# Branch A's values: split fp32r products of one head against unsplit fp32 products of two heads on the two column halves of the array

## The chip, the cores and the metric

The kernel runs on one core of one Trainium2 chip. The metric is the device time of the whole program in microseconds (us), the median of several runs. Shorter is better. The engines are TensorE (PE in the profile, its weight loads PEld), VectorE (DVE), ScalarE (ACT), GpSimd (POOL) and SyncE (SP), which here issues all transfers.

## The reference

One layer of an encoder with two token-mixing branches is applied to two groups (prompt and sample) of 1024 tokens and 1024 channels, with the same weights. Cut to what matters here:

```python
h = rms_norm(x, norm_g) * (1 + scale) + shift
qa, ka, va, za, qb, kb, vb, zb, ga, gb = split(h @ w_in)
# branch A: 8 query heads, 2 key/value heads, 64 dims each
qa, ka = rope(rms_norm(qa)), rope(rms_norm(ka))
p  = softmax(qa @ ka.T / 8)            # for each of 8 heads, 1024 x 1024
oa = (p @ va) * silu(za)               # four query heads share one va
# branch B: 4 heads, two 64-dim softmax maps each, 128-dim values
pd = softmax(q0 @ k0.T / 8) - lam * softmax(q1 @ k1.T / 8)
ob = rms_norm(pd @ vb) * (1 - lam_init) * silu(zb)
merged = sigmoid(ga) * (oa @ w_proj_a) + sigmoid(gb) * (ob @ w_proj_b)
y = x + gate * (merged @ w_out)
```

## The kernel before

Everything is fp32 in and out. Most matrix products are made of fp32r operands that were split in two: a rounded part (an ACT copy to fp32r) and the remainder (a DVE or POOL subtraction), with two or three matmuls for one product. Branch B's values (line 810) are an exception: `WHOLE` is true for both of its pairs of heads, and they use plain fp32 operands in one matmul each.

The two groups run one after the other. Each has a head (keys, values and the first queries of branch A), then six phases of attention, then gates, projections and the output. Phases 0 and 1 are branch A's heads 0 to 3 and 4 to 7, which share key/value head 0 and 1; phases 2 to 5 are branch B's heads. During a phase the attention's steps are woven with projections: `qa_gen`, `qkb_gen` and `vb_gen` (line 497) and `z_gen` (line 679), which store the gate paths. `weave` takes steps in proportion to tables of weights; a scheduler then orders each engine's instructions by simulated time and priority, and attention steps are given a raised priority.

Branch A's attention before works in **units**: one head and 256 queries, 32 units a group. A unit has two score tiles of 128 queries by 1024 keys. For each, four matmuls (lines 709 and 710) fill a double bank of PSUM, DVE takes the maximum (711), ACT the exponential into a tile p (712), of which there are four; DVE transposes p in 32 x 32 blocks (745); and four transfers (750) bring it as pieces into a tile q. So q holds the 256 queries' weights with keys on partitions; it is `pair()`, with two buffers.

The values follow `BEHIND` 1.4 units later, in `a_values`. `pT_pieces` goes over q in four pieces: ACT copies a piece to fp32r into a tile hi (758), DVE subtracts in place (759). For each of eight chunks of 128 keys there are then two matmuls of 128 x 256: va's rounded part (columns 0 to 63) and its remainder (64 to 127) are the stationary operand, hi (770) and the rest in q (771) the moving one. Rows 0 to 63 of the result a and rows 64 to 127 are summed at the end by an ACT copy of one half (786) and a DVE addition (787), and a transfer stores 64 rows (791). There is one buffer for a.

A score tile of the unit after next needs a free p, p is free when its transfers into q are done, and those wait until q is no longer read by line 771. All transfers are issued in order by SP.

Of the kernel before, what the change touches and what calls it, by code (L numbers as in the profile page):

```python
# [20 lines left out]
P = 128  # L21
T = 1024
D = 1024
NCH = D // P
# [40 lines left out]
BEHIND = 1.4  # L65
AHEAD = 100
PV_LAG = 2

WHOLE = (True, True)
# [21 lines left out]
def kernel(ctx: ExitStack, tc: tile.TileContext, t: dict):  # L91
# [8 lines left out]
    qpool = ent(tc.tile_pool(name="qpool", bufs=2))  # L100
    tpool = ent(tc.tile_pool(name="tpool", bufs=2))
# [450 lines left out]

    def pipelined(ht, w, front, back):
        pend = []
        for tt in range(NTT):
            ps = yield from proj_tt(ht, w, tt)
            pend.append((tt, front(tt, ps)))
            if len(pend) > LAG:
                back(*pend.pop(0))
            yield 1  # L560
        while pend:
            for _ in range(1 if alone[0] else 3):
                yield 1
            back(*pend.pop(0))
        yield 1
# [79 lines left out]
    def vb_gen(ht, out, pr):  # L645
        w = load_w(w_cols(w_in, (C_VB + pr * 256, 256)))
        if WHOLE[pr]:
            v = utile().bitcast(F32).rearrange("p (n h e) -> p n h e", n=NTT, h=2)
            out[2 * pr], out[2 * pr + 1] = v[:, :, 0], v[:, :, 1]
        else:  # L650
            vs = [utile().rearrange("p (n s e) -> p n s e", n=NTT, s=2) for _ in range(2)]
            out[2 * pr], out[2 * pr + 1] = vs
        for tt in range(NTT):
            ps = yield from proj_tt(ht, w, tt)
            if WHOLE[pr]:
                nc.scalar.activation(v[:, tt].rearrange("p h e -> p (h e)"), ps, AF.Copy)
                yield 1
                continue
            for i in range(2):
                vp = ps[:, i * P : (i + 1) * P]  # L660
                nc.scalar.activation(vs[i][:, tt, 0, :], vp, AF.Copy)
                nc.vector.tensor_tensor(
                    out=vs[i][:, tt, 1, :], in0=vp, in1=vs[i][:, tt, 0, :].bitcast(F32), op=ALU.subtract
                )
            yield 1
# [51 lines left out]
    def scores(u, i):  # L717

        nm_ = len(u["q"])
# [5 lines left out]
        su = u["su"][:, qt : qt + 1] if m == 0 else tiny.tile([P, 1], F32, tag="su", name=nm("su"))  # L725
        softmax_unit(u["q"][m][:, qt * P : (qt + 1) * P], u["sw"][:, m, t * P : (t + 1) * P], u["k"][m], pt, su)
        if m == 0:
# [8 lines left out]
        return t if m == nm_ - 1 else None  # L736

    def flip(u, t):


        pt = u[t][0]
        if len(u[t]) > 1:
            _, p1, f = u[t]
            nc.vector.scalar_tensor_tensor(out=pt, in0=p1, scalar=f, in1=pt, op0=ALU.mult, op1=ALU.add)
        nc.vector.transpose(pt, pt)  # L745
# [6 lines left out]
    def pT_pieces(u):  # L752

        pT = u["pT"].rearrange("p (q c b) -> p c q b", q=8, c=8)
        for cc in range(4):
            tl = pT[:, cc * 2 : cc * 2 + 2]
            th = tpool.tile([P, 2, 8, 32], F32R, tag="hi", name=nm("hi"), bufs=3)
            nc.scalar.activation(th, tl.bitcast(F32), AF.Copy)  # L758
            nc.vector.tensor_tensor(out=tl, in0=tl.bitcast(F32), in1=th.bitcast(F32), op=ALU.subtract)  # L759
            yield cc, th, tl  # L760

    def a_values(u):
        acc = ps_a.tile([P, 512], F32, tag="a", name=nm("a"))[:, :256]
        ready = []

        def pv(cc, th, tl):
            for c in range(2):
                k = cc * 2 + c
                lt = u["v"](k)
                nc.tensor.matmul(acc, lt, th[:, c, :], start=(k == 0), stop=False)  # L770
                nc.tensor.matmul(acc, lt, tl[:, c, :], start=False, stop=(k == 7))  # L771

        for piece in pT_pieces(u):
            ready.append(piece)
            if len(ready) > PV_LAG:
                pv(*ready.pop(0))
            yield 1
        while len(ready) > 1:
            pv(*ready.pop(0))
            yield 1  # L780
        pv(*ready.pop())
        tmp = mtile("at", [P, 256], bufs=1)
        o = mtile("oo", [P, 256])
        j = u["j"]
        a, b = (slice(0, 64), slice(64, 128)) if j % 2 == 0 else (slice(64, 128), slice(0, 64))
        nc.scalar.activation(tmp[a], acc[b], AF.Copy)
        nc.vector.tensor_tensor(  # L787
            out=query_order(o[a]), in0=piece_order(acc[a]), in1=piece_order(tmp[a]), op=ALU.add
        )
        pr = u["pr"]  # L790
        dma(u["od"][pr // 2][a, (pr % 2) * 256 : (pr % 2 + 1) * 256], o[a])
        yield 1

    def b_values(u):
        acc = ps_a.tile([P, 512], F32, tag="a", name=nm("a"))[:, :256]
        ready = []
        def pv(cc, th, tl):
            for c in range(2):
                k = cc * 2 + c
                for s, rt in ((0, th), (0, tl), (1, th)):  # L800
                    nc.tensor.matmul(
                        acc, u["v"][:, k, s, :], rt[:, c, :],
                        start=(k == 0 and s == 0 and rt is th), stop=(k == 7 and s == 1),
                    )

        if WHOLE[u["h"] // 2]:
            pT = u["pT"].bitcast(F32).rearrange("p (q c b) -> p c q b", q=8, c=8)
            yield 1
            for k in range(NCH):
                nc.tensor.matmul(acc, u["v"][:, k], pT[:, k], start=(k == 0), stop=(k == 7))  # L810
                if k % 2:
                    yield 1
        else:
            for piece in pT_pieces(u):
                ready.append(piece)
                if len(ready) > PV_LAG:
                    pv(*ready.pop(0))
                yield 1
            while len(ready) > 1:
                pv(*ready.pop(0))  # L820
                yield 1
            pv(*ready.pop())
# [20 lines left out]
    def attention(units):  # L843
# [11 lines left out]
        for at, ph, n, i, qk in steps:  # L855
# [4 lines left out]
            with tc.high_priority(offset=AHEAD):  # L860
# [12 lines left out]
                if t is not None:  # L873
                    late.append(lambda u=live[n], t=t: flip(u, t))
                    if t == (0 if ph < 2 else 0) and n + 1 < len(units) and units[n + 1][2]():
# [140 lines left out]
    def units_of(st):  # L1016

        def a_unit(half, i, pr):
            j = half * 4 + i
            kv = j // 4  # L1020
            return {
                "q": [st["qa"][half][i % 2][:, i // 2]], "k": [st["ka"][:, kv]],
                "v": (lambda k: st["va"][:, k, kv, :]),
                "pr": pr, "j": j, "od": st["od"][j // 2], "su": st["suA"][:, j],
# [14 lines left out]
        for half in range(2):  # L1039
            units += [  # L1040
                (half, lambda a=(half, i, pr): a_unit(*a), lambda a=("qa", half, pr): there(*a))
                for i in (0, 2, 1, 3) for pr in range(4)
# [29 lines left out]
    for g in range(2):  # L1072
# [11 lines left out]
        def phase(k, *fs, more=()):  # L1084
            n_att = 16 * (6 + PV_LAG) if k < 2 else 4 * (9 + PV_LAG)
# [96 lines left out]
```

## Time and profile before

| | |
|---|---|
| median of 3 runs (lowest, highest) | 1984.54 us (1979.33, 1988.07) |
| span of the profiled execution | 1985.5 us, which is also the only time that the profile gives for it |
| mean granted TensorE clock | 0.982 |
| DMA | 295.11 MB, mean 149 GB/s |

A row of the profile's groups reads: line, engine, operation, output and inputs by the program's names, shapes and types, the count; then busy time in us and the mean of one in ns; then the time for which the engine was idle just before such instructions and what it waited for. Busy time counts overlapping instructions once. A matmul's duration contains its way through the array, so that two in a row overlap; how fast they follow one another is read from their starts or ends. In a row of the waits stand who waited for whom, the total in us, how often, and the longest.

Where PE's time goes, beside the lines shown with the prediction (busy us of the groups): line 679 582.3, line 497 487.0, lines 709 and 710 (scores) together 421.2, line 950 (projections after the gates) 187.2, line 979 (output) 178.6.

### The profile page before, as it was taken

How to read it: one execution, taken by the hardware profiler on the slowest of the kernel's cores; microseconds unless marked ns; L12 is line 12 of the kernel's file. 1: busy time of each engine (PE TensorE's matmuls, PEld its weight loads, DVE VectorE, ACT ScalarE, POOL GpSimd, SP SyncE). 2: the span in 40 equal slices, each digit the busy share in tenths (PEclk: the TensorE clock that was granted, in tenths of full speed). 3: DMA queues.
4: the chain of work that ended last, by engine and by line, in shares of the span. 5: the costliest groups of instructions: out<-in, count | busy, mean ns of one | idle time of the engine just before them, and what ended most of it. 6: DMA issues, size and time to landing. Idle time of an engine off the chain costs nothing.

```text
span 1985.5 us, 30670 instructions
## 1 busy us (share of the span) xinstructions
PE 1908.6 (96%) x10466; PEld 1627.8 (82%) x10466; DVE 1330.8 (67%) x1906; ACT 1009.9 (51%) x1939; POOL 758.1 (38%) x1008
## 2 busy tenths in 40 slices
PE   8889999999999998999999899999999999999999
PEld 3878888888878994778888787888887888877887
DVE  4558877777877577547465877677788845665641
ACT  4435655665654444754323565556655534566310
POOL 2374612453446252221235464134445626422110
PEclk9899999999999999999999999999999999999999
DMA  8124556555553345865641455565654333567532
GB/s 310 33 80 126 155 152 169 152 166 154 133 153 102 101 120 173 257 227 167 222 149 35 140 144 145 149 164 144 184 137 137 106 97 99 156 212 245 174 101 75
DMA packets 269531, 295.11 MB, mean 149 GB/s; under 512 B 35776, under 2 KB 218176, under 8 KB 269376
## 3 DMA queue, kind: packets, MB, share of 16 engines
q1 hardware_dynamic: 269376, 293.15, 49.7%
q8 instruction: 84, 1.38, 0.3%
q14 instruction: 71, 0.58, 0.1%
HBM read 133.59 MB, written 42.01 MB: 88 GB/s over the span
## 4 chain that ended last, share of the span: by engine, by line
PE 68%; DMA 8%; DVE 8%; ACT 5%; SPq 4%; issue 3%; POOL 3%; ACTq 0%; POOLq 0%; DVEq 0%
PE f L497 16%; PE f L679 16%; PE f L950 6%; PE f L979 5%; PE s L709 4%; PE a L810 4%; PE s L710 4%; PE s L979 4%; DMA q<-p 3%; SPq L750 3%; PE s L950 2%; DVE q L759 2%; PE a L771 2%; PE a L770 2%; DVE m L711 2%
## 5 line engine op out<-in xcount | busy, mean ns | idle before, releaser
L679 PE MATMUL f<-u,w 128*128 128x512 f32 x2232 | 582.3, 398 | 0.1
L497 PE MATMUL f<-w,u 128*128 128x256 f32 x3456 | 487.0, 286 | 2.2 <-ACT ev L685 1.4
L497 PEld LDWEIGHTS f<-w,u 128*128 128x128 f32 x3456 | 459.5, 192 | 22.4 <-ACT ev L685 1.8
L679 PEld LDWEIGHTS f<-u,w 128*128 128x128 f32 x2232 | 408.8, 190 | 77.3 <-POOL w L181 0.8
L181 POOL TENSOR_TENSOR w<-st,w 128x512 fp32r<-128x512 f32 x168 | 230.3, 1390 | 439.9 <-ACT w L179 375.1
L712 ACT ACTIVATE p<-s,m 128x1024 f32<-128x1024 f32 x256 | 284.4, 1111 | 206.3 <-DVE m L711 111.3
L711 DVE TENSOR_REDUCE m<-s 128x1 f32<-128x1024 f32 x256 | 310.0, 1216 | 51.3 <-PE s L710 48.7
L745 DVE STREAM_TRANSPOSE p<-p 128x1024 f32<-128x1024 f32 x192 | 238.2, 1241 | 99.2 <-ACT p L712 86.5
L759 DVE TENSOR_TENSOR q<-q,hi 128x512 fp32r<-128x512 f32 x256 | 198.3, 792 | 60.6 <-ACT hi L758 58.6
L515 POOL TENSOR_TENSOR rs<-ss,nhalf 128x4 f32<-128x4 f32 (+1 forms) x112 | 112.8, 1007 | 322.8 <-DVE ss L514 284.0
L758 ACT ACTIVATE hi<-q 128x512 fp32r<-128x512 f32 x256 | 153.8, 625 | 104.1 <-DMA q<-p 55.4
L710 PE MATMUL s<-u,sw 128*128 128x512 f32 x512 | 206.7, 404 | 0.0
L179 ACT ACTIVATE w<-st 128x512 fp32r<-128x512 f32 x196 | 113.9, 625 | 97.2 <-DMA st<-in_w_in_dram 46.0
L950 PE MATMUL f<-u,w 128*128 128x512 f32 x552 | 133.4, 395 | 5.1 <-ACT ev L685 4.4
L770 PE MATMUL a<-hi,u 128*128 128x256 f32 x512 | 132.5, 285 | 2.1 <-DVE oo L787 2.1
L771 PE MATMUL a<-q,u 128*128 128x256 f32 x512 | 129.8, 286 | 1.2 <-DVE q L759 1.2
L810 PE MATMUL a<-q,u 128*128 128x256 f32 x512 | 128.3, 390 | 1.9 <-DVE oo L826 1.5
L950 PEld LDWEIGHTS f<-u,w 128*128 128x128 f32 x552 | 103.9, 190 | 27.2 <-ACT ev L685 4.7
L709 PE MATMUL s<-u 128*128 128x512 f32 x256 | 110.9, 433 | 15.1 <-ACT p L712 15.1
L810 PEld LDWEIGHTS a<-q,u 128*128 128x128 f32 x512 | 97.8, 196 | 17.5 <-DVE oo L826 1.6
L709 PE MATMUL s<-u,u 128*128 128x512 f32 x256 | 103.6, 405 | 8.3 <-ACT p L712 7.7
L710 PEld LDWEIGHTS s<-u,sw 128*128 128x128 f32 x512 | 98.4, 192 | 15.5
(175 smaller groups left out, 2562.1 us busy)
## 6 DMA issues: line engine op xcount, KB each, us to landing
q<-p SPq DMA_DIRECT2D x768, 128.0 KB, 2.6
st<-in_w_in_dram SPq DMA_DIRECT2D x132, 256.0 KB, 3.0
zd<-ev SPq DMA_DIRECT2D x96, 256.0 KB, 2.2
sw<-u SPq DMA_DIRECT2D x256, 64.0 KB, 2.1
p<-zd SPq DMA_DIRECT2D x64, 256.0 KB, 3.2
u<-in_w_ada_dram SPq DMA_DIRECT2D x8, 1024.0 KB, 10.4
st<-in_w_in_dram SPq DMA_DIRECT2D x64, 128.0 KB, 2.7
st<-in_w_out_dram SPq DMA_DIRECT2D x32, 256.0 KB, 2.9
```

Source lines behind the costliest of these rows:

```text
L181: e.tensor_tensor(out=wl, in0=st, in1=wh.bitcast(F32), op=ALU.subtract)
L497: nc.tensor.matmul(ps, lt[c][:, sl], w[:, c, wi, :], start=(k == 0), stop=(k == 23))
L679: nc.tensor.matmul(ps, w[:, c, wi, e * P : (e + 1) * P], rt[c], start=(k == 0), stop=(k == 23),)
L709: nc.tensor.matmul(s[:, sl], q, k[:, sl], start=True, stop=False)
L710: nc.tensor.matmul(s[:, sl], sw, k[:, sl], start=False, stop=True)
L711: nc.vector.tensor_reduce(out=m, in_=s, axis=AX.X, op=ALU.max, negate=True)
L712: nc.scalar.activation(pt.rearrange("p (j c a) -> p j c a", j=4, c=8), s.rearrange("p (c a j) -> p j c a", c=8, j=4), AF.Exp, bias=m, accu ...
L745: nc.vector.transpose(pt, pt)
L759: nc.vector.tensor_tensor(out=tl, in0=tl.bitcast(F32), in1=th.bitcast(F32), op=ALU.subtract)
L810: nc.tensor.matmul(acc, u["v"][:, k], pT[:, k], start=(k == 0), stop=(k == 7))
L950: nc.tensor.matmul(ps, w[:, c, wi, d * P : (d + 1) * P], o[:, oi, :], start=(k == 0), stop=(k == 11))
L979: nc.tensor.matmul(ps, w[:, c, wi, e * P : (e + 1) * P], m[:, mi, :], start=(k == 0), stop=(k == 23))
```

## The change

Branch A's attention works in **couples** of units: two neighbouring query heads that share a key/value head, and 256 queries; 16 couples a group. A couple has four score tiles, two for each head, and a q tile for each head. There are three q buffers; the pool of hi is gone.

va is kept as plain fp32. A couple's result a has one head in rows 0 to 63 and the other in rows 64 to 127. For each of the eight chunks there are two matmuls with 64 columns of va as stationary operand and 256 columns of the one or the other head's q as moving operand, in fp32 without a split. The 16 are emitted in turn between the halves, and `together` binds them: each after the first gets a very high priority and a dependence, without a semaphore, on the one before it. The result is copied by one ACT instruction of 128 rows and stored by one transfer.

The path for split weights in branch B, which `WHOLE` had switched off, is deleted with its flag; branch B's instructions stay. Steps of the values in phases 0 and 1 become two for a couple (`PAIRS`: 1.05 couples behind, 0.3 apart over both), and the counts that `weave` divides by follow.

```diff
+PAIRS = (1.05, 0.3)
+TOP = 100000
-PV_LAG = 2
-WHOLE = (True, True)
...
-    qpool = ent(tc.tile_pool(name="qpool", bufs=2))
-    tpool = ent(tc.tile_pool(name="tpool", bufs=2))
+    qpool = ent(tc.tile_pool(name="qpool", bufs=3))
...
+    def behind(ins, other):
+        dep = mybir.DependencyInfo(mybir.DependencyClass.NoSync, mybir.DependencyReason.DATA)
+        tc.add_manual_dep(ins.ins, other.ins.name, dep)
+
+    def together(calls):
+
+        prev = None
+        for call in calls:
+            if prev is None:
+                ins = call()
+            else:
+                with tc.high_priority(offset=TOP):
+                    ins = call()
+                behind(ins, prev)
+            prev = ins
...
-        va = utile().rearrange("p (n k d) -> p n k d", n=NTT, k=2)
+        va = utile().bitcast(F32)[:, :1024].rearrange("p (n k d) -> p n k d", n=NTT, k=2)
...
-            vt = va[:, tt]
-            nc.scalar.activation(vt[:, :, 0:64], vp, AF.Copy)
-            nc.vector.tensor_tensor(out=vt[:, :, 64:128], in0=vp, in1=vt[:, :, 0:64].bitcast(F32), op=ALU.subtract)
+            nc.scalar.activation(va[:, tt], vp, AF.Copy)
...
-        t, m = i // nm_, i % nm_
+        pairs = "h" not in u
+        t, m = (i % 2, i // 2) if pairs else (i // 2, i % 2)
...
-            u["pT"] = pair(F32R)
-        dst = u["pT"].bitcast(F32).rearrange("p (i t f) -> p i t f", i=4, t=2)
+            pT = pair()
+            if "h" in u:
+                u["pT"] = pT
+            else:
+                u.setdefault("pT", []).append(pT)
+        dst = (u["pT"] if "h" in u else u["pT"][m]).rearrange("p (i t f) -> p i t f", i=4, t=2)
...
-    def pT_pieces(u):
-            nc.scalar.activation(th, tl.bitcast(F32), AF.Copy)
-            nc.vector.tensor_tensor(out=tl, in0=tl.bitcast(F32), in1=th.bitcast(F32), op=ALU.subtract)
...
     def a_values(u):
         acc = ps_a.tile([P, 512], F32, tag="a", name=nm("a"))[:, :256]
-                nc.tensor.matmul(acc, lt, th[:, c, :], start=(k == 0), stop=False)
-                nc.tensor.matmul(acc, lt, tl[:, c, :], start=False, stop=(k == 7))
...
-        nc.scalar.activation(tmp[a], acc[b], AF.Copy)
-        nc.vector.tensor_tensor(
-            out=query_order(o[a]), in0=piece_order(acc[a]), in1=piece_order(tmp[a]), op=ALU.add
-        )
+        pT = [x.rearrange("p (q c b) -> p c q b", q=8, c=8) for x in u["pT"]]
+        together([
+            lambda k=k, m=m: nc.tensor.matmul(
+                acc[(LO, HI)[m]], u["v"][:, k], pT[m][:, k], start=(k == 0), stop=(k == 7)
+            )
+            for k in range(NCH) for m in (1, 0)
+        ])
+        yield 1
         o = mtile("oo", [P, 256])
+        nc.scalar.activation(query_order(o), piece_order(acc), AF.Copy)
...
-            na, nv = (2, 4 + PV_LAG) if ph < 2 else (4, 5 + PV_LAG)
-            steps += [(n + i / na, ph, n, i, True) for i in range(na)]
-            steps += [(n + BEHIND + i / nv, ph, n, i, False) for i in range(nv)]
+            nv, after, pace = (2, *PAIRS) if ph < 2 else (7, BEHIND, 1.0)
+            steps += [(n + i / 4, ph, n, i, True) for i in range(4)]
+            steps += [(n + after + i * pace / nv, ph, n, i, False) for i in range(nv)]
...
-            n_att = 16 * (6 + PV_LAG) if k < 2 else 4 * (9 + PV_LAG)
+            n_att = 8 * 6 if k < 2 else 4 * 11
```

How PE's order changes at the first values of the first group. A row is line, operation, result and inputs with the numbers of their buffers (a is the values' result, f a projection's, u a kept tile, here va in u_397 and u_394, w a weight), output shape, and a count of equal rows in turn. Before, the middle of the first unit's 16 matmuls:

```order
L679 MATMUL f_1504<-u_553,w_1346 128x512
L771 MATMUL a_1568<-q_1546,u_397 128x256
L770 MATMUL a_1568<-hi_1569,u_397 128x256
L771 MATMUL a_1568<-q_1546,u_397 128x256
L770 MATMUL a_1568<-hi_1599,u_397 128x256
L679 MATMUL f_1504<-u_553,w_1346 128x512
L771 MATMUL a_1568<-q_1546,u_397 128x256
L770 MATMUL a_1568<-hi_1599,u_397 128x256
L771 MATMUL a_1568<-q_1546,u_397 128x256
L770 MATMUL a_1568<-hi_1616,u_397 128x256
```

And now, the start of the first couple's 16 (q_1610 is the second head's tile, q_1537 the first's; twelve more rows like the last two follow before the next score tile):

```order
L679 MATMUL f_1493<-u_548,w_1335 128x512 x2
L679 MATMUL f_1493<-u_549,w_1335 128x512
L679 MATMUL f_1493<-u_548,w_1335 128x512
L768 MATMUL a_1649<-q_1610,u_394 64x256
L768 MATMUL a_1649<-q_1537,u_394 64x256
L768 MATMUL a_1649<-q_1610,u_394 64x256
L768 MATMUL a_1649<-q_1537,u_394 64x256
```

Before, a projection's matmul stands between pieces, and hi and q take turns within one head; now the two heads' matmuls take turns on the two halves of a with nothing between.

On ACT at the same place before (hi are the rounded pieces of two units' q tiles, p the exponentials, at the copy of one half of a):

```order
L758 ACTIVATE hi_1623<-q_1546 128x512
L712 ACTIVATE p_1706,suA_117<-s_1708,m_1707 128x1024
L758 ACTIVATE hi_1683<-q_1573 128x512
L758 ACTIVATE hi_1715<-q_1573 128x512
L509 ACTIVATE row_1636<-f_1514 128x256
L510 ACTIVATE row_1636<-row_1636 128x256
L685 ACTIVATE ev_1692<-f_1504 128x512
L758 ACTIVATE hi_1723<-q_1573 128x512
L786 ACTIVATE at_1677<-a_1568 64x256
L712 ACTIVATE p_1737,suA_117<-s_1739,m_1738 128x1024
```

And now, up to the first couple's eviction:

```order
L712 ACTIVATE p_1615,suA_114<-s_1617,m_1616 128x1024
L712 ACTIVATE p_1699,suA_114<-s_1701,m_1700 128x1024
L508 ACTIVATE row_1585<-f_1503 128x256
L509 ACTIVATE row_1585<-row_1585 128x256
L712 ACTIVATE p_1736,suA_114<-s_1738,m_1737 128x1024
L685 ACTIVATE ev_1635<-f_1493 128x512
L775 ACTIVATE oo_1677<-a_1649 128x4x2x32
L712 ACTIVATE p_1759,suA_114<-s_1761,m_1760 128x1024
```

The pieces between the exponentials are gone, with the DVE subtractions that followed them, and one copy of full height writes the result.

More of the change, by code (lines that the diff above doesn't have):

```diff
@@ L724, in scores @@
         pt = ptile()
-        su = u["su"][:, qt : qt + 1] if m == 0 else tiny.tile([P, 1], F32, tag="su", name=nm("su"))
+        if pairs:
+            su = u["su"][:, m, qt : qt + 1]
+        else:
+            su = u["su"][:, qt : qt + 1] if m == 0 else tiny.tile([P, 1], F32, tag="su", name=nm("su"))
         softmax_unit(u["q"][m][:, qt * P : (qt + 1) * P], u["sw"][:, m, t * P : (t + 1) * P], u["k"][m], pt, su)
+        if pairs:
+            u[m, t] = [pt]
+            return m, t
         if m == 0:
@@ L735, in scores, with flip @@
             u[t] += [pt, f]
[L736 to L743, printed above, removed]
+        return (0, t) if m else None
+    def flip(u, mt):
+        m, t = mt
+        if "h" in u:
+            mt = t
+        pt = u[mt][0]
+        if len(u[mt]) > 1:
+            _, p1, f = u[mt]
             nc.vector.scalar_tensor_tensor(out=pt, in0=p1, scalar=f, in1=pt, op0=ALU.mult, op1=ALU.add)
@@ L746, in flip @@
         if t == 0:
-            u["pT"] = pair(F32R)
-        dst = u["pT"].bitcast(F32).rearrange("p (i t f) -> p i t f", i=4, t=2)
+            pT = pair()
+            if "h" in u:
+                u["pT"] = pT
+            else:
+                u.setdefault("pT", []).append(pT)
+        dst = (u["pT"] if "h" in u else u["pT"][m]).rearrange("p (i t f) -> p i t f", i=4, t=2)
         for i in range(4):
             dma(dst[:, i, t], pt[i * 32 : i * 32 + 32])
-    def pT_pieces(u):
[L754 to L760, printed above, removed]
@@ L795, in b_values @@
         acc = ps_a.tile([P, 512], F32, tag="a", name=nm("a"))[:, :256]
[L796 to L817, printed above, removed]
+        pT = u["pT"].rearrange("p (q c b) -> p c q b", q=8, c=8)
+        yield 1
+        for k in range(NCH):
+            nc.tensor.matmul(acc, u["v"][:, k], pT[:, k], start=(k == 0), stop=(k == 7))
+            if k % 2:
                 yield 1
[L819 to L822, printed above, removed]
         sq = mtile("at", [P, 256], bufs=1)
@@ L1016, in units_of, with a_unit @@
     def units_of(st):
-        def a_unit(half, i, pr):
-            j = half * 4 + i
-            kv = j // 4
+        def a_unit(half, b, pr):
+            kv = half
+            j = half * 4 + 2 * b
             return {
-                "q": [st["qa"][half][i % 2][:, i // 2]], "k": [st["ka"][:, kv]],
-                "v": (lambda k: st["va"][:, k, kv, :]),
-                "pr": pr, "j": j, "od": st["od"][j // 2], "su": st["suA"][:, j],
+                "q": [st["qa"][half][i][:, b] for i in range(2)], "k": [st["ka"][:, kv]] * 2,
+                "v": st["va"][:, :, kv, :],
+                "pr": pr, "od": st["od"][j // 2], "su": st["suA"][:, j : j + 2],
             }
@@ L1040, in units_of @@
             units += [
-                (half, lambda a=(half, i, pr): a_unit(*a), lambda a=("qa", half, pr): there(*a))
-                for i in (0, 2, 1, 3) for pr in range(4)
+                (half, lambda a=(half, b, pr): a_unit(*a), lambda a=("qa", half, pr): there(*a))
+                for b in range(2) for pr in range(4)
             ]
```

41 lines of the change are left out of this document (5 added, 36 removed).

## The prediction

> **What bounds the kernel now.** I read the page's totals first, then busy time by stretch, then the rows of the lines that the diff touches, then the waits inside the two stretches where branch A's attention runs.
>
> ```profile
> span 1985.5 us, 30670 instructions
> PE 1908.6 (96%) x10466; PEld 1627.8 (82%) x10466; DVE 1330.8 (67%) x1906; ACT 1009.9 (51%) x1939; POOL 758.1 (38%) x1008
> ...
> PE 68%; DMA 8%; DVE 8%; ACT 5%; SPq 4%; issue 3%; POOL 3%; ACTq 0%; POOLq 0%; DVEq 0%
> ...
> L758 ACT ACTIVATE hi<-q 128x512 fp32r<-128x512 f32 x256 | 153.8, 625 | 104.1 <-DMA q<-p 55.4
> L759 DVE TENSOR_TENSOR q<-q,hi 128x512 fp32r<-128x512 f32 x256 | 198.3, 792 | 60.6 <-ACT hi L758 58.6
> L770 PE MATMUL a<-hi,u 128*128 128x256 f32 x512 | 132.5, 285 | 2.1 <-DVE oo L787 2.1
> L771 PE MATMUL a<-q,u 128*128 128x256 f32 x512 | 129.8, 286 | 1.2 <-DVE q L759 1.2
> ```
>
> PE is busy for 96% of the span and holds 68% of the chain that ended last. The change touches lines 758 to 787, which run in branch A's attention: 150 to 550 us in the first group, 1100 to 1510 in the second. By stretch (PE, PEld, DVE, ACT, POOL busy, then the granted clock):
>
> ```profile
> 150.00:550.00 400.00, 397.38 (x2357) 350.25 (x2355) 308.25 (x398) 239.30 (x476) 164.12 (x210) 1.00 0.55 152
> 1100.00:1510.00 410.00, 398.00 (x2343) 349.97 (x2342) 318.14 (x412) 247.54 (x489) 171.89 (x223) 0.99 0.55 152
> ```
>
> Here PE is idle for 2.6 and 12.0 us, and a clock of 0.99 costs some 4 us in the second stretch: 19 us is all that PE loses to others in both. DVE has over 90 us of room in each and ACT 160. So work taken from DVE and ACT is not worth its own time. The change pays by what it does to PE's own time, plus whatever part of those 19 us it frees.
>
> **PE's time, removed.** The 1024 matmuls of lines 770 and 771. Their cost is the distance from one to the next, not the mean of 285 ns, which contains the pipeline. Twelve in turn:
>
> ```profile
> 409.41 0.28 PE L770 MATMUL a<-hi,u 128*128 128x256 f32 x1
> ...
> 410.71 0.28 PE L771 MATMUL a<-q,u 128*128 128x256 f32 x1
> ```
>
> Eleven steps in 1.30 us are 0.118 us each; 1024 of them are 120.8 us.
>
> **PE's time, added.** 32 couples of 16 fp32 matmuls with 256 columns of moving data. The profile shows such a matmul as two passes: line 810 (branch B's values, fp32 already) has 256 matmuls in the program and 512 records.
>
> ```profile
> 568.60 1.46 PE L810 MATMUL a<-q,u 128*128 128x256 f32 x6
> L810 PE MATMUL a<-q,u x512: 377/379/634, 555.9 to 1811.9; 128*128 128x256 f32 x171
> ```
>
> Six passes last 1.46 us and one alone 0.379, so the step is (1.46 - 0.38) / 5 = 0.216 us. The new ones use 64 columns of the array. Narrower is not faster for the pass itself, as the two-column matmuls of line 435 show below. There are 1024 passes, 512 on each half. Whether the halves run side by side, no row of this trace shows, for none uses a second part of the array. The ends are: all in series, 1024 x 0.216 = 221 us; fully side by side, 111 us. I take side by side, since the two halves have their own columns, their own rows of the result and their own moving data, and the built program alternates them without anything between. In order, a matmul's two passes must follow each other on their half, so the sequence is a, a and b, a and b and so on: 17 pass times for a couple, 17 x 0.216 = 3.67 us, 117.5 us in all.
>
> [...]
>
> Entering and leaving the narrow mode costs something. [...]
>
> ```profile
> 751.80 0.82 PE L548 MATMUL f<-ident,row 128*128 128x128 f32 x4
> 752.55 2.74 PE L435 MATMUL f<-st,cT 128*2 128x512 f32 x6
> 755.22 0.50 PE L709 MATMUL s<-u 128*128 128x512 f32 x1
> 755.55 0.40 PE L710 MATMUL s<-u,sw 128*128 128x512 f32 x1
> ...
> 761.19 0.39 PE L710 MATMUL s<-u,sw 128*128 128x512 f32 x1
> 761.51 1.02 PE L435 MATMUL f<-st,cT 128*2 128x512 f32 x2
> ```
>
> Counted from end to end, six of them take 2.67 us (752.62 to 755.29) and two take 0.95 (761.58 to 762.53). So one takes 0.43, which is 0.215 for each 256 columns of moving data, as at full width, and going in costs 0.95 - 0.86 = 0.09. Coming out, the next matmul ends 0.43 after them where its follower needs 0.23: 0.20. With 0.29 for each of 32 couples that is 9.3 us. It is paid once a couple only because nothing stands between the 16. The bounds are nothing and, if loading 64 columns shows at the entrance more than two do, twice that.
>
> On PE the change therefore costs 117.5 + 9.3 - 120.8 = **+6 us**.
>
> [...]
>
> **Off PE.** Gone are 256 copies on ACT (153.8 us) and 256 subtractions on DVE (198.3), and of the evictions:
>
> ```profile
> L786 ACT ACTIVATE at<-a 64x256 f32<-64x256 f32 x64 | 24.2, 378 | 1.5
> L787 DVE TENSOR_TENSOR oo<-a,at 64x256 f32<-64x256 f32 x64 | 26.7, 418 | 1.1
> ```
>
> 64 additions go and the 64 copies become 32 of full height. None of this is on PE, so it counts only through waits. In the two stretches (first group, then second) the matching rows are:
>
> ```profile
> PE s L709 <- ACT p L712: 1.4, 3, 1.0
> PE a L771 <- DVE q L759: 0.3, 1, 0.3
> ACT p L712 <- DMA q<-p: 44.6, 23, 5.2
> SPq L750 <- PE a L771: 32.1, 17, 3.5
> ...
> PE s L709 <- ACT p L712: 6.4, 7, 2.1
> PE a L770 <- DVE oo L787: 2.1, 1, 2.1
> PE a L771 <- DVE q L759: 0.9, 1, 0.9
> ACT p L712 <- DMA q<-p: 38.9, 21, 5.5
> SPq L750 <- PE a L771: 56.0, 23, 6.1
> ```
>
> The waits on the split and the addition (0.3 + 2.1 + 0.9 = 3.3 us) lose their cause. The score matmuls' waits on the exponential (1.4 + 6.4 = 7.8) hang on it at one remove: ACT waits for a free p tile, whose transfer into q stands on SP behind the values matmuls that still read q. The old path had two more steps after landing, 0.63 on ACT and 0.79 on DVE, four times a unit, and two q tiles; now there are none and three tiles. I let these 7.8 go too, and 3 of the 4 us of lost clock, which follow the idle time: **-14 us**, bounded by nothing (other waits take their place) and the 19 us above.
>
> What is late next: the block needs all eight transfers of each head, and whatever stands behind it on PE waits with it. From a score tile to landed pieces the trace has
>
> ```profile
> L711 DVE TENSOR_REDUCE m<-s 128x1 f32<-128x1024 f32 x256 | 310.0, 1216 | 51.3 <-PE s L710 48.7
> L712 ACT ACTIVATE p<-s,m 128x1024 f32<-128x1024 f32 x256 | 284.4, 1111 | 206.3 <-DVE m L711 111.3
> L745 DVE STREAM_TRANSPOSE p<-p 128x1024 f32<-128x1024 f32 x192 | 238.2, 1241 | 99.2 <-ACT p L712 86.5
> ...
> L750 SPq DMA_DIRECT2D q<-p x768: 542/602/2098, 154.3 to 1801.3; - x192
> ...
> q<-p SPq DMA_DIRECT2D x768, 128.0 KB, 2.6
> ```
>
> 1.2 + 1.1 + 1.2 + 4 x 0.6 + 2.6 = 8.5 us. In the new program PE has 10 to 22 us of other work, at this trace's steps, between a couple's last score tile and its block, in all 16 couples of the first group. So the block should rarely wait; I charge nothing, and if that cover were gone it would cost up to some microseconds a couple. The third q tile takes the space of hi. Branch B, which uses q tiles too, keeps its steps, so I count nothing there, though every engine's order after the first block moves somewhat: the ends of the range allow for that.
>
> **Sum.** The profiled execution spans 1985.5 us, 1 us over the runs' median of 1984.54; no further time around the span is shown. 1985.5 + 6 - 14 = 1977.5, so 1977 us, 0.4% under the median. For this case the range is 1962 (entering free, all 19 us gone) to 1992 (no wait freed).
>
> **Rivals.**
> The halves don't run side by side. For it: no row shows that they do. Against it: separate columns and separate results. Then the block is 32 x 0.216 + 0.29 = 7.2 us, 230.5 us in all, +110 and -14: 2081 us. It decides soon. With waits freed as above, the change breaks even where the mean step of a pass is (120.8 + 14 - 9.3) / 1024 = 0.1226 us against the 0.115 of my case, so little may be lost.
>
> They overlap only in part, for instance only where the second pass of one matmul meets the first of the next: three pass times for four, a step of 0.162, 175 us in all, 2026 us. Anything down to the break-even belongs here, from 1990 upward. [...]
>
> More goes than I let go. Score tiles come in closer pairs without splits between them on ACT and DVE, and waits outside these lines (transposes, evictions) shrink as well; with the entrance hidden too: 1955 to 1962 us.
>
> The block holds PE up. A couple's transfers come later than planned because SP's queue is in order and a transfer waits there for a q tile that the previous block frees; half a microsecond a couple is 16 us: 1993. The 8.5 us against at least 10 speak against it.
>
> That the 16 are not in turn can be excluded: the built program has all 32 blocks whole, the first two matmuls of each with the only waits.
>
> **How the numbers follow.** My case 0.58, in series 0.10, partly 0.10, more gained 0.16, PE held up 0.06. A difference of 0.5% is about what a measurement of this kernel can tell from none. Faster by over that is below 1974.6: all of the third rival and 0.4 of my case, 0.39. Slower is above 1994.5: the first two, half of the last and a twentieth of my case, 0.26. Within: 0.35. The range, 1952 to 2012, takes in my case, the gain beyond it and the block that holds PE up, and the near end of partial overlap; in series and most of the rest of partial overlap stay outside.
>
> **What would show it.** The new matmuls' row: a block's 32 records spanning about 3.9 us end to end means side by side, about 7 in series, 5 to 6 partly. The first matmul after a block ending 0.2 us late shows the way out. PE's idle time in the two attention stretches should fall below 5 us from 14.6. ACT's waits on q transfers there should fall well below 83 us. If the block is whole and short and the time is still not below 1985, the lost microseconds stand as idle time before the block or as a lower clock.

## The result, and the profile after

| | before | after |
|---|---|---|
| median of 4 runs each (lowest, highest) | 1983.11 us (1979.33, 1988.07) | 1966.37 us (1965.58, 1970.28) |
| span of the profiled execution | 1985.5 us | 1968.4 us |
| mean granted TensorE clock | 0.982 | 0.983 |

The change is faster: the ratio is 0.9922, with a 95% interval of 0.9900 to 0.9943, some 17 us. The two profiled executions differ by 17.1 us in span.

The page of after, with its totals, the shares of the chain that ended last, and the groups that answer to those shown of before (line 768 is the new matmul, 711 the maximum, 712 the exponential, 753 the transpose that was line 745):

```profile
span 1968.4 us, 29657 instructions
PE 1900.2 (97%) x10466; PEld 1574.4 (80%) x10466; DVE 1110.0 (56%) x1570; ACT 861.2 (44%) x1653; POOL 723.6 (37%) x1008
...
PE 81%; DMA 6%; ACT 3%; POOL 3%; DVE 3%; issue 2%; SPq 2%; ACTq 0%; POOLq 0%; DVEq 0%
...
L711 DVE TENSOR_REDUCE m<-s 128x1 f32<-128x1024 f32 x256 | 310.2, 1219 | 240.6 <-PE s L710 238.5
L712 ACT ACTIVATE p<-s,m 128x1024 f32<-128x1024 f32 x256 | 285.1, 1114 | 241.3 <-DVE m L711 208.8
L753 DVE STREAM_TRANSPOSE p<-p 128x1024 f32<-128x1024 f32 x192 | 237.3, 1240 | 70.3 <-ACT p L712 61.7
L768 PE MATMUL a<-q,u 128*64 128x256 f32 x1024 | 117.7, 382 | 0.8 <-DMA q<-p 0.8
```

DVE has lost 221 us of work and ACT 149, and the program has become 17 us shorter. PE's share of the chain has risen from 68 to 81%, and DVE's has fallen from 8 to 3%: there is less to wait for, but PE was the bound before, too.

The first blocks of the values in the timeline of PE (start, duration, instruction, records), and the score matmuls behind the first:

```profile
168.80 1.08 PE L679 MATMUL f<-u,w 128*128 128x512 f32 x4
169.81 3.67 PE L768 MATMUL a<-q,u 128*64 128x256 f32 x32
173.41 0.50 PE L709 MATMUL s<-u,u 128*128 128x512 f32 x1
173.75 0.40 PE L710 MATMUL s<-u,sw 128*128 128x512 f32 x1
...
186.37 3.67 PE L768 MATMUL a<-q,u 128*64 128x256 f32 x32
```

Counted as the prediction counts, from end to end, a block takes 173.48 - 169.88 = 3.60 us, and the next matmul ends 173.91 - 173.48 = 0.43 later, where its follower takes 0.24 (the raw ends give 0.429 and 0.235). That is 3.80 us for a couple, the block and the way out of it, 121.6 us for 32, against the 120.8 us of the matmuls removed. On PE the change is worth **+1 us**.

Busy time in the two stretches of branch A's attention (length; PE, PEld, DVE, ACT, POOL busy; granted clock), and behind each the stretch of branch B's that follows:

```profile
150.00:550.00 400.00, 399.34 (x2380) 328.46 (x2380) 217.93 (x252) 169.30 (x340) 142.88 (x207) 1.00 0.55 155
550.00:860.00 310.00, 288.12 (x1517) 236.82 (x1516) 188.71 (x270) 157.69 (x287) 124.86 (x191) 0.97 0.53 157
1100.00:1510.00 410.00, 405.01 (x2394) 333.31 (x2393) 229.92 (x269) 181.16 (x361) 162.25 (x232) 0.99 0.57 158
1510.00:1800.00 290.00, 275.14 (x1495) 238.74 (x1494) 179.53 (x255) 154.37 (x276) 117.39 (x178) 0.96 0.50 149
```

In branch A's stretches PE is idle for 0.7 + 5.0 = 5.7 us instead of 14.6. Branch B's values now start some 30 us earlier, at 525 and 1476 us, so the ends of these stretches already hold some of branch B. The waits in them (who waited for whom, us, how often, the longest; first stretch, then second):

```profile
ACT p L712 <- DVE m L711: 69.7, 39, 5.4
ACT p L712 <- DMA q<-p: 14.0, 7, 4.1
PE s L709 <- ACT p L712: 0.5, 2, 0.3
...
PE s L709 <- ACT p L712: 2.9, 3, 2.5
ACT p L712 <- DMA q<-p: 2.8, 2, 2.0
PE a L768 <- DMA q<-p: 0.8, 1, 0.8
```

ACT's exponential waited 83.5 us for transfers into q, and now 16.8. What it waits for instead is the maximum (line 711), and that waits for PE's next score tile: of the idle time before the maxima, 48.7 us were laid to the scores before, and now 238.5. ACT and DVE have become engines that wait for PE.

Over the whole program, the time from the end of one of the 10466 passes to the end of the next, above the median step of its kind, was 122.0 us before. It is 116.3 after, of which 32 x 0.34 = 11 are the entries and exits of the blocks (a narrow pass counted as 0.108). So PE waits some 17 us less. This count sees more than idle time does: the records of matmuls overlap (in after's first block most last 0.38 us and their pairs start 0.216 us apart), so a short wait leaves no idle time between them. By what waited (after without the entries and exits of the blocks):

| lost by PE above the median step (us) | before | after |
|---|---|---|
| score matmuls (lines 709, 710) | 37.1 | 27.9 |
| transposes (line 548, now 547) | 24.5 | 17.1 |
| branch A's values | 7.4 | 0.9 |
| branch B's values (line 810, now 785) | 7.1 | 14.1 |
| all others | 45.9 | 45.2 |

Cut at the ends of each group's first and last score matmul, with the first output matmul as a third mark, the 17 us fall so:

| stage (us) | before | after |
|---|---|---|
| head of group 1 | 149.8 | 146.7 |
| attention of group 1 | 667.3 | 666.9 |
| gates and projections, group 1 | 122.5 | 123.5 |
| output of group 1, head of group 2 | 164.8 | 162.0 |
| attention of group 2 | 682.3 | 670.2 |
| gates, projections and output, group 2 | 198.8 | 199.1 |

In the first group the attention gains nothing: what branch A no longer waits comes back in branch B. Its largest piece is one wait in the stretch from 550 to 860 us. The same kind of wait came to 0.4 us there before (last line, from the waits of before):

```profile
735.69 0.61 PE L797 MATMUL f<-ones_c,at 128*128 128x1 f32 x4
741.75 3.75 PE L785 MATMUL a<-q,u 128*128 128x256 f32 x8 [5.46 <-DMA q<-p]
...
PE a L810 <- DMA q<-p: 0.4, 1, 0.4
```

Every other kernel below has this wait too, with 5.2 to 5.9 us, in units as in couples. So it is not a price of the couples or of the narrow products; what brings it was not found.

### The profile page after: what moved, and what is told of

Read it like the earlier page. It is cut to its first block, busy times and chain, and to the rows that moved or that the text cites. A ratio compares the mean times of both kernels' runs of the same rounds, so it can differ in the third digit from the quotient of the medians.

```text
span 1968.4 us, 29657 instructions
## 1 busy us (share of the span) xinstructions
PE 1900.2 (97%) x10466; PEld 1574.4 (80%) x10466; DVE 1110.0 (56%) x1570; ACT 861.2 (44%) x1653; POOL 723.6 (37%) x1008
## 4 chain that ended last, share of the span: by engine, by line
PE 81%; DMA 6%; ACT 3%; POOL 3%; DVE 3%; issue 2%; SPq 2%; ACTq 0%; POOLq 0%; DVEq 0%
PE f L679 21%; PE f L496 19%; PE f L915 6%; PE a L768 6%; PE f L944 5%; PE s L709 5%; PE s L710 5%; PE s L944 4%; PE a L785 4%; PE s L915 2%; DMA row<-zd 1%; SPq L762 1%; DMA st<-in_w_in_dram 1%; PE f L547 1%; DMA q<-p 1%
## 5 line engine op out<-in xcount | busy, mean ns | idle before, releaser
L679 PE MATMUL f<-u,w 128*128 128x512 f32 x2232 | 579.3, 398 | 1.7 <-ACT w L178 1.2
L711 DVE TENSOR_REDUCE m<-s 128x1 f32<-128x1024 f32 x256 | 310.2, 1219 | 240.6 <-PE s L710 238.5
L180 POOL TENSOR_TENSOR w<-st,w 128x512 fp32r<-128x512 f32 x168 | 220.9, 1332 | 456.4 <-ACT w L178 410.9
L915 PE MATMUL f<-u,w 128*128 128x512 f32 x552 | 134.6, 398 | 4.4 <-ACT ev L685 3.7
L785 PE MATMUL a<-q,u 128*128 128x256 f32 x512 | 130.2, 393 | 7.3 <-DMA q<-p 5.5
L550 DVE TENSOR_TENSOR u<-f,u 64x256 fp32r<-64x256 f32 (+1 forms) x196 | 80.4, 411 | 71.3 <-ACT u L549 66.4
L768 PE MATMUL a<-q,u 128*64 128x256 f32 x1024 | 117.7, 382 | 0.8 <-DMA q<-p 0.8
L944 PE MATMUL f<-u,w 128*128 128x512 f32 x456 | 105.6, 389 | 0.0
L508 ACT ACTIVATE row<-f 128x256 f32<-128x256 f32 (+1 forms) x112 | 41.1, 367 | 146.1 <-PE f L496 135.5
```

The lines of the kernel that those rows point to most:

```text
L180: e.tensor_tensor(out=wl, in0=st, in1=wh.bitcast(F32), op=ALU.subtract)
L679: nc.tensor.matmul(ps, w[:, c, wi, e * P : (e + 1) * P], rt[c], start=(k == 0), stop=(k == 23),)
L711: nc.vector.tensor_reduce(out=m, in_=s, axis=AX.X, op=ALU.max, negate=True)
L768: lambda k=k, m=m: nc.tensor.matmul(acc[(LO, HI)[m]], u["v"][:, k], pT[m][:, k], start=(k == 0), stop=(k == 7))
L915: nc.tensor.matmul(ps, w[:, c, wi, d * P : (d + 1) * P], o[:, oi, :], start=(k == 0), stop=(k == 11))
L944: nc.tensor.matmul(ps, w[:, c, wi, e * P : (e + 1) * P], m[:, mi, :], start=(k == 0), stop=(k == 23))
```

## The experiments

**One: before without the split.** Both products read q itself, so the remainder's product is replaced by a second one of q. Units, their matmuls and the additions stay.

```diff
-            th = tpool.tile([P, 2, 8, 32], F32R, tag="hi", name=nm("hi"), bufs=3)
-            nc.scalar.activation(th, tl.bitcast(F32), AF.Copy)
-            nc.vector.tensor_tensor(out=tl, in0=tl.bitcast(F32), in1=th.bitcast(F32), op=ALU.subtract)
-            yield cc, th, tl
+            yield cc, tl, tl
```

> The kernel before, with one edit: branch A's q pieces are not split; both matmuls of a chunk read q itself (the output is not the reference's: the remainder product is replaced by a second rounded one). PE has the same 1024 matmuls, the unit order and two q tiles stay. Theory 1 (the gain is PE's waits that hung on the splits on ACT and DVE): most of the gain appears here, 1966 to 1973 us, with PE's idle time in the two attention stretches of A down from 14.6 to about 6 us. Theory 2 (the gain is a better program order of couples, or chance of the order): 1980 to 1986. Theory 3 (the third q tile): 1980 to 1986.

1977.79 us, ratio 0.9990 (0.9974 to 1.0007). PE's idle time in the two stretches, by the same view, has fallen nearly as far as after's, to 2.4 + 5.4 us:

```profile
150.00:550.00 400.00, 397.58 (x2360) 353.20 (x2360) 229.08 (x278) 175.35 (x355) 145.02 (x209) 1.00 0.57 156
1100.00:1510.00 410.00, 404.65 (x2380) 356.86 (x2378) 236.69 (x295) 183.53 (x370) 161.10 (x227) 0.99 0.57 157
```

Yet the program gains at most 5 us. A stretch's idle time is no measure of the program's gain. By the ends of its passes, PE lost less in this run at the scores (30.2 us), the transposes (17.9) and branch A's values (0.7), nearly as in after, but at branch B's values 17.8 us where before had 7.1: 10.7 us of what was freed came back as waits there.

**Two: after with dummies for the split's work.** Eight ACT copies and eight DVE subtractions a couple, on constant data.

```diff
+    def as_split(u, n):
+        for i in range(n):
+            h = u["vx"][:, i % 2]
+            x = ident.unsqueeze(1).to_broadcast([P, 4, P])
+            nc.scalar.activation(h, x, AF.Copy)
+            nc.vector.tensor_tensor(out=h, in0=x, in1=h.bitcast(F32), op=ALU.subtract)
```

> The changed kernel, with eight copies on ACT and eight subtractions on DVE of 128 x 512 added for each couple, as many as the split had, but on data that nothing waits for. Theory 1 in its form 'busy time of ACT and DVE': back up by 8 to 15 us, to 1975 to 1982. Theory 1 in its form 'two more steps in the chain from transfer to matmul', theory 2 and theory 3: within 4 us of 1966.

2038.45 us, ratio 1.0288 (1.0269 to 1.0307). This says nothing of the split: with no operand to wait for, the scheduler moved the dummies forward. The busy tenths of DVE in 40 slices show it, in slices 2 to 5 and again in 22 to 25 (this run, then after):

```profile
DVE  5999973345477466646479998544518745666641
...
DVE  5557762444667466647464667444447735665641
```

**Three: after with two q tiles** instead of three (`bufs=2`).

> The changed kernel with two q tiles in place of three. Theory 3 (the third tile): back to 1976 or above, the transfers into q waiting on SP for the values' matmuls. Theories 1 and 2: within 5 us of 1966, since PE has 10 us or more of other work between a couple's last score tile and its block.

1967.44 us, ratio 0.9935 (0.9917 to 0.9952). The third tile is worth nothing that can be measured.

**Four: after without the binding** of the 16 matmuls.

```diff
-                with tc.high_priority(offset=TOP):
-                    ins = call()
-                behind(ins, prev)
+                ins = call()
```

> The changed kernel with the 16 matmuls of a couple emitted without the binding and the high priority. In the built program the blocks fall into 40 runs in place of 32, with 472 changes of half in place of 480. By the cost of a block's entry and exit in the changed kernel's trace (0.14 + 0.20 us), 8 more of them are 3 us: 1967 to 1971. If the binding itself carries the gain: 1976 or above.

1972.43 us, ratio 0.9957 (0.9941 to 0.9974), 6 us over after. The blocks are cut into 40 pieces instead of 32; eight more entries and exits are 8 x 0.34 = 2.7 us. By their ends the pieces with their exits take 126.9 us, where after's blocks take 122.5, so 4.4 us are theirs: a piece of one matmul takes its two pass times alone (0.576 us with the entry), with nothing on the other half. What is left of the 6 us is less than another order can make.

**Five: eight matmuls of one half, then eight of the other.**

```diff
-            for k in range(NCH) for m in (1, 0)
+            for m in (1, 0) for k in range(NCH)
```

> The changed kernel with the same 16 matmuls, first the eight of one half, then the eight of the other. If the halves run side by side only because matmuls of different halves alternate: a block of 32 x 0.216 + 0.34 = 7.25 us in place of 3.80, 32 blocks, +110 us, 2070 to 2085. If the engine finds work for the other half further down its queue: no change, 1966.

2052.8 us in the one run, with before at 1981.65. The first block in the timeline of PE:

```profile
169.38 6.32 PE L768 MATMUL a<-q,u 128*64 128x256 f32 x32
175.62 0.50 PE L709 MATMUL s<-u,u 128*128 128x512 f32 x1
```

End to end a block takes 6.25 us, 28 pass times of 0.216 and some 0.2, not 32 pass times. By the raw records, a pass that starts at 172.026, 5 ns after the 13th, lasts 0.43 us like the first of the block, where the others last 0.38, and three more run beside the 14th to 16th. The records don't name the half; the pass at 172.026 is read here as the first of the second half, and by that reading this half started four passes, two matmuls, ahead of its place in this block. The blocks are 199.8 - 116.2 = 84 us longer than after's, the program 86.

**Six: couples with fp32r at full width.** Couples, binding and three q tiles stay; va is split and q is rounded without its remainder, whose products are replaced by a second product of q. A couple has 32 matmuls of 128 x 256 in place of 16 narrow ones, and two copies of 64 rows take the result out; the two halves of va's products are not added.

```diff
-                acc[(LO, HI)[m]], u["v"][:, k], pT[m][:, k], start=(k == 0), stop=(k == 7)
+                acc[:, m * 256 : m * 256 + 256], u["v"][:, k], pT[m][:, k],
+                start=(k == 0 and i == 0), stop=(k == 7 and i == 1),
...
-            for k in range(NCH) for m in (1, 0)
+            for m in (1, 0) for k in range(NCH) for i in range(2)
```

> The changed kernel's couples, binding and three q tiles, but full-width fp32r matmuls as before: for each head 16 of 128 x 256 in turn, q unsplit in both, the two heads in two halves of the bank's columns; the sum of the rounded and the remainder half of va is left out, so the output is not the reference's. PE's block costs 32 x 0.118 = 3.8 us, as the narrow one does. Theory 1a (halves only pay for what the splits' absence and the couples bring): the same as the changed kernel, 1963 to 1970. Theory 1b (the narrow halves are themselves faster on PE than the trace's steps say): 1975 or above, near the unsplit units' 1978.

1971.18 us, ratio 0.9942 (0.9923 to 0.9962), which overlaps after's. Its first block:

```profile
165.33 4.02 PE L770 MATMUL a<-q,u 128*128 128x256 f32 x32
169.18 0.40 PE L711 MATMUL s<-u,u 128*128 128x512 f32 x1
```

The next matmul ends at 169.58, 0.23 after the block, so nothing is paid on leaving. From the end of the matmul before it (165.49 by the raw ends) the block takes 3.86 us, where the narrow block with its exit takes 3.80. Over all couples that is 123.9 us against 122.5: for PE the two are nearly the same. So most of the gain doesn't hang on the narrow products.

**Seven: after with the split's work at its time.** The same eight copies and subtractions as in the second run, but they read q; nothing reads their result.

```diff
+        for cc in range(4):
+            x = q[:, cc * 2 : cc * 2 + 2].bitcast(F32)
+            h = u["vx"][:, cc % 2]
+            nc.scalar.activation(h, x, AF.Copy)
+            nc.vector.tensor_tensor(out=h, in0=x, in1=h.bitcast(F32), op=ALU.subtract)
```

> The changed kernel, with the eight copies on ACT and eight subtractions on DVE for each couple reading the couple's q tiles, as the split did and at its time, into a scratch tile that nothing reads. Theory 1 (ACT's and DVE's work in the attention of A makes PE wait): up by 5 to 15 us, to 1971 to 1981, with more idle time of PE in 150 to 550 and 1100 to 1510 us. Theory 2 (only the plan of couples matters): within 3 us of 1966.

1988.48 us, ratio 1.0035 (1.0022 to 1.0048): 22 us over after, more than either theory allowed, and above before. By the same view of the two stretches, and the groups of the copies and subtractions:

```profile
150.00:550.00 400.00, 393.61 (x2321) 322.43 (x2320) 301.17 (x371) 233.10 (x458) 150.04 (x200) 0.99 0.55 153
1100.00:1510.00 410.00, 398.81 (x2352) 327.23 (x2351) 314.35 (x389) 241.26 (x477) 171.70 (x216) 0.99 0.55 152
...
L773 DVE TENSOR_TENSOR u<-q,u 128x512 fp32r<-128x512 f32 x256 | 194.9, 792 | 59.4 <-ACT u L772 45.6
L772 ACT ACTIVATE u<-q 128x512 fp32r<-128x512 f32 x256 | 152.0, 625 | 117.2 <-DMA q<-p 59.6
```

DVE and ACT carry what they carried before (308 and 318 us, 239 and 248), and PE is idle for 6.4 + 11.2 = 17.6 us again, though no matmul waits for these instructions' results. The work need not be on PE's path. ACT stood idle for 59.6 us before the copies until a transfer into q had landed, and an exponential behind a copy in ACT's order waits with it. PE's score matmuls waited for the exponential for 5.1 + 4.5 us (after: 0.5 + 2.9):

```profile
PE s L711 <- ACT p L714: 5.1, 4, 2.4
...
PE s L711 <- ACT p L714: 4.5, 5, 2.5
```

By the ends of the passes, the profiled execution lost 16 us more than after's, 9.5 of them at the score matmuls, 4.0 at branch A's values and 3.2 at the transposes.

**Eight and nine: the same work in another order.** `PAIRS` (1.3, 0.3) places a couple's values later behind its scores; (1.05, 0.6) draws its two steps apart.

> The changed kernel with its values a quarter of a couple later (PAIRS 1.3 in place of 1.05), the same work in another order. It measures what another plan of the same work is worth by itself: by theory 1 within 5 us of 1966; if the gain is the luck of an order, as much as 10 us or more worse.

> As after, with the two steps of a couple's values 0.6 couples apart in the plan instead of 0.3 over both, so that the result's copy and store come later in the order; nothing else changes. Theory (the order of the same work is worth up to 9 us either way, as the plan with 1.3 showed): anywhere within 1960 to 1976 us, the 32 blocks unchanged at 3.6 us. Rival (only the distance of the block from its score tiles matters, and that stays): 1965 to 1970 us.

1975.84 us, ratio 0.9965 (0.9950 to 0.9981), and 1970.79 us, ratio 0.9942 (0.9922 to 0.9963). The order alone is worth up to 9 us; none of the orders tried beats after's.

**Ten: two chunks of one half, then two of the other.**

```diff
-            for k in range(NCH) for m in (1, 0)
+            for kk in range(0, NCH, 2) for m in (1, 0) for k in (kk, kk + 1)
```

> As after, but the 16 matmuls of a block change half only after every second one: two chunks of one half, then the same two of the other. Theory one (PE runs strictly in order, with one pass of each half under way at most, so that a half's pass can only run beside the next in the program if that one is the other half's; the eight-by-eight order showed 6.25 us for one block, 28 or so pass times for 32): of the 8 passes of a group of four matmuls, those at the three changes of half in it meet a neighbour, the others are alone. A block then has about 3 of 4 pass times, 24 to 26 x 0.216 + 0.14 = 5.3 to 5.8 us, and the program is 54 to 70 us slower than after: 2020 to 2036 us. Theory two (a queue of several instructions looks ahead past the ones that wait for their half): a block stays at 16 to 18 pass times, 3.6 to 4.0 us, and the program at 1966 to 1980 us.

1970.31 us in the one run. The first block:

```profile
169.14 3.73 PE L768 MATMUL a<-q,u 128*64 128x256 f32 x32
172.80 0.50 PE L709 MATMUL s<-u,u 128*128 128x512 f32 x1
```

3.65 us end to end, 0.05 more than in turn. The pass that is read as the second half's first, fifth in the program, starts 13 ns after the first half's. So here the third matmul in the program started with the first, two places ahead; in the fifth run, by the same reading, the second half's first matmul, the ninth, started with the seventh. Turns of two cost next to nothing (0.05 us a block) and turns of eight 84 us.

**Eleven and twelve: without the split, in two other orders.** The first run's kernel with branch A's values 1.2 and 1.6 units behind the scores instead of 1.4.

> Before without the split (th and tl are both q itself, so the remainder's product is replaced by a second one of q), as in the earlier run that gained only 4 us, and in addition the values of branch A are planned 1.2 units behind the scores instead of 1.4. Theory (removing the split frees PE some 10 to 15 us, and the earlier run's order happened to give most of it back): 1966 to 1974 us here or in the run with 1.6. Rival (in units, without couples, the freed work of ACT and DVE is worth no more than about 4 us): 1976 to 1982 us here and there.

> The same kernel without the split, with the values of branch A planned 1.6 units behind the scores instead of 1.4. Theory (the order gave most of the gain back): 1966 to 1974 us here or in the run with 1.2. Rival (in units the gain is about 4 us whatever the order): 1976 to 1982 us here and there. If it is over 1984 us, a q tile that stays in use longer holds the transfers back, and the distance matters as well.

1977.31 us, ratio 0.9977 (0.9960 to 0.9994), and 1978.23 us, ratio 0.9980 (0.9961 to 0.9999). The small gain of the first run was no accident of its one order: in units, the split's removal is worth 2 to 5 us in the three orders (by the intervals, nothing to 8).

## Why the prediction was right, and where its terms were not

**The time.** 1977 us was forecast and 1966 measured: inside the range, and 8 us beyond the 1974.6 from which a gain counts as over 0.5%. The likeliest case held in its mechanism (halves side by side, PE about even, waits gone), with the time near the lower end of its own range of 1962 to 1992. But the gain that its sum gave was 8 us and the measured one is 17. Both terms were too cautious, by 5 us on PE and by 3 to 4 in the waits, and the width of the range took that in. The prediction gave a gain of over 0.5% a chance of 0.39 and its own 1977 us lay outside of that, so the side on which it came out was in part luck.

**PE's term, +6 us, was +1.** The step of 0.216 us and the exit of 0.20 came as taken. Two parts were mis-sized. The sequence was counted as "a, a and b, a and b and so on", 17 pass times for a couple; in after's first block the two halves start 7 ns apart from the first pair, so there are 16. The count took it that no matmul starts before the one ahead of it has begun its last pass; that was the author's estimate, which no run shows: in after the second matmul's first pass starts those 7 ns behind the first's. And going in cost 0.144 us (3.60 - 16 x 0.216) instead of 0.09. The first is -6.9 us over 32 couples, the second +1.7.

**In series, and partly.** Both rivals are out for the order that was built: 6.25 and 3.60 us are the blocks of the two orders. The sum had no term of its own for weight loads. The loads of after's blocks, by the groups:

```profile
L768 PEld LDWEIGHTS a<-q,u 128*64 128x64 f32 x1024 | 71.8, 137 | 40.1 <-issue 6.1 <-DMA q<-p 1.0
```

1024 loads of 137 ns would be 140 us by themselves, more than the 121.6 us of the blocks with their exits. In after's trace all but 0.03 us of these 140 lies inside the time that PE's matmul records cover, so the loads ran beside passes.

**The waits, -14 us, were -17 to -18, and not for the reasons named alone.** The first part held: waits on the split and the addition are gone (3.3 us, with 0.8 for a transfer in their place). Of the score matmuls' 7.8 us, 3.4 stayed, so 4.4 went. The 3 us of clock can't be found: the mean granted clock went from 0.982 to 0.983, at most 2 us, and in the second stretch it was 0.99 both times, with 12.0 and 5.0 us of idle time. Named terms thus make 7 to 9 us; PE's idle time in the two stretches fell by 8.9, to 5.7 where "below 5" was foretold. The reading that failed is that 19 us of idle time and clock are all that PE loses to others there. By the ends of the passes it lost 27.7 us in the two stretches before, and after 23.4, of which 11 are the entries and exits of the blocks: some 15 less. So the 14 us are close to what these stretches gave, with some 6 us of it in what idle time doesn't show (after's stretches also hold some of branch B). Outside of them the prediction counted nothing, and there two things nearly cancel: the head and the part between the groups became 3 us shorter each, and other waits of scores and transposes shrank, as the rival "more goes than I let go" had it of waits outside its lines, while branch B's values lost 7 us more.

**What the waits hang on.** Seven shows that the split's work on ACT and DVE, put back at its time, takes all of the gain away. One, eleven and twelve show that its removal alone gives only 2 to 5 us. Six shows that couples without the split and without narrow products have 11 (its interval is 8 to 15). So the gain is that of both together, and the price of the work in couples (22 us) is more than what it cost in units. That may be because a couple's eight pieces come at once and a unit's four by themselves, or because the copies of run seven share two scratch tiles where hi had three: ACT waited 15.9 us for a subtraction before them, and 1.2 us before the split's. Neither was tried. What in the couples (fewer evictions, blocks without projections between them, another order) is worth the 7 us or more that units without the split lack, the runs don't settle, since an order alone moves the time by as much. After's order is also the best of those tried, which lie between 1966 and 1976 us, so up to 9 of its 17 us can hang on the order.

**The rest.** The block was to wait rarely: one of 32 did, 0.75 us at 1220 us. That cover held. The third q tile "takes the space of hi": it isn't needed. The slower rival, a block that holds PE up, did not come, though a wait for q of 5.5 us in branch B is of its kind; the kernels in units without the split have it as well.

## What to carry to other kernels

Here fp32 products of 64 columns for two heads, in turn on the two halves of the array, cost PE as much as split fp32r products at full width (121.6 us in after, 120.8 us in before), and they spare the split on the other engines; so the question is what those engines' work costs, and that is asked by putting it back at its time, reading the operand that it read. In the seventh run work whose results PE never reads still cost the program 22 us through what stands behind it. Before a gain of half a per cent is put down to a part, the same work should be run in another order: here that alone moved 9 us.

## What the runs showed of the hardware

In turn, in after, the passes of the two column halves started in pairs, 5 to 8 ns apart, and a pair followed a pair in 0.216 us (0.27 behind the first of a block). That holds for 31 of the 32 blocks; in the one that waited, at 1220 us, all pairs were 126 ns apart. In the fifth and tenth run passes that are read as the second half's first started up to two matmuls (four passes) ahead of their place in the program; there the starts lie 5 to 58 ns apart. Entering a block of 64 columns took 0.14 us and leaving it 0.20 (after's first block), where two columns took 0.09 and 0.20 (line 435 of before).
